# Sums of moving operands kept in DRAM, fewer plain blocks at an operand change, and a split that comes two steps after its fetch

## The chip, the core and the metric

The kernel runs on one core of one Trainium2 chip. The metric is the device time of one execution in microseconds (us); the time quoted for a kernel is the median of several executions. All matrix products are made by TensorE (PE), which reads both operands from on-chip memory and writes to PSUM; VectorE (DVE), ScalarE (ACT) and GpSimd (POOL) do the rest; SyncE (SP) issues nearly all DMA transfers, in one queue and in order.

## The reference, cut to what matters

One transformer-like layer over 2048 tokens of width 1024, all in float32: a token mixer, a cross-attention into 256 memory tokens, and a SwiGLU feed-forward part, each between two RMS norms.

```python
def reference(x, mem, w_in, sinks, ...):
        ...
        y = jnp.concatenate([ya, yh.astype(ya.dtype)], axis=-1) @ w_out[l]
        h = h + rms_norm(y, g_mix_post[l])
        u = rms_norm(h, g_x_pre[l])
        m = rms_norm(mem, g_mem[l])
        y = cross_attention(u, m, wq_x[l], wk_x[l], wv_x[l], wo_x[l])
        h = h + rms_norm(y, g_x_post[l])
        u = rms_norm(h, g_ffn_pre[l])
        y = (jax.nn.silu(u @ w_gate[l]) * (u @ w_up[l])) @ w_down[l]
        h = h + rms_norm(y, g_ffn_post[l])
```

The lines shown are those that the changed stage computes; the input projection, the sliding-window attention and the recurrence come before it and are not touched.

## The kernel before

Every float32 operand is split into a high and a low part, and a product is made of three matmuls (high by high, high by low, low by high; L950, L951 and L952). The high part is a rounding copy on ACT (L870), the low part a subtraction on DVE (L873).

The later part of the kernel is a chain of eight *jobs* (`jobs`, L1158). A job is one matrix product whose *moving* operand (called T here) stays the same while a row of *blocks* runs over tokens or columns. A block is a product of a 2x2 arrangement of stationary tiles S with the 2x2 arrangement of T, 256 rows by 1024 columns of output. The jobs in order, with the names used below:

| name | moving operand from | k tiles per quarter (`nk`) | blocks |
|---|---|---|---|
| w_out | the output projection | 4 | 8 |
| qk | `qk_d`, a folded product of weights | 4 | 8 |
| vo | `vo_d`, another one | 4 | 8 |
| u0, u1 | `u_d`, the normed tokens 0 to 1023, then 1024 to 2047 | 4 | 22 each |
| d0, d1, d2 | `w_down`, in three parts | 3, 4, 4 | 8 each |

A block is made in one of two ways (`STEPS`, L863). A *plain* block ("p", function `eight`) makes the eight quarter products from the four quarters of T, under the keys 1, 2, 8 and 3. An "s" block (function `seven`) makes the same output from seven products; its T operands are the quarters 1, 2 and 3 and four sums of quarters, under the keys 5, 7, 6 and 4, used in the order 1, 5, 6, 3, 7, 2, 4. One product is 3 x `nk` matmuls into one PSUM bank; it is called a step below.

`kinds` (L1180) makes the first block of every job plain (the first two of w_out) and the last one too, but for the very last block of the kernel. Between jobs the T operands must be exchanged: there are seven slots for them in on-chip memory (L1045), and a slot is free when its operand was used for the last time. Since the last block of a job is plain, the slots of the four sums come free before it, and the four quarters' slots during it. `half` (L1063) is called after every step of a block (twice after a step of a plain block) and makes half an operand: in `resident` (L875) it fetches one or two tiles of 512 KB into *row* tiles (nine of them for all uses, `row_tile`, L1196), for a sum makes a `tensor_tensor` on DVE (L887 for key 5, L890 for 7, L893 for 6, L896 for 4), and splits the result on ACT and DVE (L870, L873). Keys 6 and 4 reuse the sum made for 7 and 6, and key 7 is taken out of turn, five steps early (L1044), for that. So nine operands are made at a change: the quarter 8 for the old job's last block, the four quarters of the new job's plain block, and the four sums.

All this is traced in the order of the Python code; a scheduler then orders the instructions of each engine, so that a split may stand earlier or later among the others than it was written. Each engine takes its instructions strictly in that order: an instruction that waits holds up all that stand behind it. SP's queue holds the loads of T, the loads of S (`streamed`, L903), and the stores of results. In w_out, vo, d1 and d2 a result tile is first added to by an accumulating DMA that POOL issues (`add`), and its store on SP waits for that transfer.

Of the kernel before, what the change touches and what calls it, by code (L numbers as in the profile page):

```python
# [11 lines left out]
F32 = mybir.dt.float32  # L12
# [3 lines left out]
ALU = mybir.AluOpType  # L16
AX = mybir.AxisListType

P = 128
T = 2048  # L20
D = 1024
# [4 lines left out]
NFF = DFF // P  # L26
# [3 lines left out]
NT = T // P  # L30
# [18 lines left out]
class Layer:  # L49
# [27 lines left out]
    def store(self, dst, src):  # L77
        self.nc.sync.dma_start(dst, src)

    def gain(self, ap):  # L80
        self._n += 1
        g = self.gp.tile([P, D], F32, tag="g", name=f"g_{self._n}")
        self.load(g, ap[0:1, :].broadcast_to([P, D]))
        return g
# [316 lines left out]
    def in_first(self):  # L401

        nc, I = self.nc, self.I
# [12 lines left out]
        T, raw = {}, {}  # L416
# [47 lines left out]
        def fetch():  # L464
            for s in range(2):
                for q in range(2):
# [9 lines left out]
                  for i, p in enumerate(self.ORDER)]  # L476
        phases = self.phases([(lambda i, j, a, n: raw[i, j][:, a:a + n, :], 4, blocks)], T)
        next(phases)
# [395 lines left out]

    def resident(self, get, nk, key, dst, keep):  # L875


        nc = self.nc
        halves = [(0, (nk + 1) // 2), ((nk + 1) // 2, nk)]

        src = []
        for h, (a, b) in enumerate(halves):
            if key in self.BLOCK:
                t = get(*self.BLOCK[key], a, b - a)
            elif key == 5:
                t, o = get(0, 1, a, b - a), get(0, 0, a, b - a)
                nc.vector.tensor_tensor(t, t, o, ALU.subtract)  # L887
            elif key == 7:
                t, o = get(1, 1, a, b - a), get(0, 1, a, b - a)
                nc.vector.tensor_tensor(t, t, o, ALU.subtract)  # L890
            elif key == 6:
                t, o = keep[7][h], get(0, 0, a, b - a)
                nc.vector.tensor_tensor(t, t, o, ALU.add)  # L893
            else:
                t = get(1, 0, a, b - a)
                nc.vector.tensor_tensor(t, t, keep[6][h], ALU.subtract)  # L896
            self.split2(t, dst[:, 0, a:b], dst[:, 1, a:b], "A")
            src.append(t)
            yield
        if key in (6, 7):  # L900
            keep[key] = src

# [128 lines left out]
    def phases(self, jobs, first, prologue=None):  # L1031

        steps = [(n, i, p) for n, (_, nk, blocks) in enumerate(jobs) for i, b in enumerate(blocks)
                 for p in self.STEPS[b[0]]]
        takes = [c for _, _, blocks in jobs for b in blocks for c in self.TAKES[b[0]]]
        need = list(itertools.accumulate(takes)) + [sum(takes)] * 2
# [8 lines left out]
        current = [None, 0]  # L1047
        if first:
            for i, p in enumerate(first):
                k = (0, p, False)  # L1050
                queue.remove(k)
                T[k] = first[p]
                slots[i] = ("A", uses[k][-1], i)

        def fetch(n, tile):
            def get(i, j, a, c):
                t = tile().rearrange("p (k d) -> p k d", d=512)[:, :c]
                jobs[n][0](t, i, j, a, c)
                return t

            return jobs[n][0] if first else get

        def half(g, tile):  # L1063

            if current[0] is None:
# [12 lines left out]
                T[k] = dst  # L1078
                current[:] = [self.resident(fetch(n, tile), jobs[n][1], p, dst, keep[n]), 0]
            next(current[0])  # L1080
            current[1] += 1
            if current[1] == 2:
                next(current[0], None)
                current[0] = None
            return True

        blocks = [b for _, _, bl in jobs for b in bl]
        streams, ready, made = [], [], [0]
# [15 lines left out]
        if not first:  # L1104
            for i in range(8):
                half(-1, prologue)
                yield
        stream(0)
# [6 lines left out]
        at = 0  # L1115
        for n, (_, nk, bl) in enumerate(jobs):
            for i, (kind, _, out, follow, addend) in enumerate(bl):
                stream(at + 1)
                cur = {}
                for q in range(g, g + len(self.STEPS[kind])):  # L1120
                    key = (n, steps[q][2], i > len(bl) // 2 if steps[q][2] == 8 else 0)
                    while key not in T or (current[0] is not None and key == list(T)[-1]):
                        assert half(q - 1, self.row_tile), (q, steps[q], queue[:3], slots)
                    cur[steps[q][2]] = T[key]
                run = (self.seven(ready, cur, nk, out, addend) if kind == "s" else
                       self.eight(ready, cur, nk, out, addend, kind == "q"))
                for q in range(len(self.STEPS[kind])):
                    next(run)
                    upto(need[g + 2])
                    for _ in range(1 if kind == "s" else 2):  # L1130
                        for f in list(after):
                            if next(f, after) is after:
                                after.remove(f)
                        half(g, self.row_tile)
                    g += 1
                after.append(follow())
                at += 1
# [20 lines left out]
    def jobs(self):  # L1158
# [24 lines left out]
        jobs = [(w_out, 4, kinds([self.mixed_block(n) for n in range(0, NT, 2)], 2)),  # L1183
                (weights(self.qk_d, 0, 4), 4, kinds([self.score_block(n) for n in range(0, NT, 2)])),
                (weights(self.vo_d, 0, 4), 4, kinds([self.value_block(n) for n in range(0, NT, 2)]))]
        for b in range(NB):
            jobs.append((ffn_u(b), 4, kinds([blk for f in range(0, NFF, 2) for blk in self.hidden_blocks(b, f)])))
        for c, (f0, nk) in enumerate(((0, 3), (6, 4), (14, 4))):
            jobs.append((weights(I["w_down"], f0 * P, nk), nk,
                         kinds([self.down_block(c, f0, nk, n) for n in range(0, NT, 2)])))  # L1190
        k, s, o, f, a = jobs[-1][2][-1]
# [122 lines left out]
    def value_block(self, n):  # L1314
# [3 lines left out]
        def out(i, j, a, b):  # L1318
            if not y:
                ss.append(self.small("q_s", 4))  # L1320
            if i not in y:
                y[i] = self.row_tile()
                if n == 0 and len(y) == 1:
                    self.g_x_post = self.gain(self.I["g_x_post"])
                    self.g_ffn_pre = self.st_pool.tile([P, D], F32, name="g_ffn_pre", bufs=1)
                    self.load(self.g_ffn_pre, self.I["g_ffn_pre"][0:1, :].broadcast_to([P, D]))
# [157 lines left out]
```

## Time and profile before

| | us |
|---|---|
| median of 3 executions | 2679.54 (2676.87 to 2679.78) |
| the profiled execution | 2676.9 |
| its span, first to last instruction | 2675.0 |
| TensorE busy in it | 2587.2 (97%) |
| VectorE busy | 1688.1 (63%) |
| ScalarE busy | 1239.6 (46%) |
| GpSimd busy | 489.3 (18%) |

The profile is a page on one execution and a trace that can be asked for views. In a row of a *view of windows* stand the stretch (us from the start), its length, then the busy time of PE, of PE's weight loads, of DVE, ACT and POOL with the number of instructions in brackets, the granted TensorE clock (1.00 is full speed), the busy share of the 16 DMA engines (slightly over 1 is possible) and GB/s. In a row of a *view of groups* stand line, engine, operation, names and shapes, the count, busy us, the mean ns of one, and the idle time of the engine before them. A busy PE is not a PE at its peak: matmuls overlap in the records, so the number of matmuls in a stretch says more than its busy time.

### The profile page before, as it was taken

To read this page: it belongs to the slowest core of one execution; us is meant where nothing else is said; L and a number is where in the kernel's file an instruction comes from. 1 tells how busy PE (TensorE), PEld (TensorE's weight loads), DVE (VectorE), ACT (ScalarE), POOL (GpSimd) and SP (SyncE) were. 2 spreads that over 40 slices of the span, in tenths; PEclk is the share of its full clock that TensorE was granted. 3 is DMA by queue.
4 is the path that set the end of the run, shared out by engine and by line. 5 is a ranking of instruction groups with operands and counts; after the bars stand their busy time and mean duration, and the time that the engine had idled before them with its cause. 6 is when DMAs were issued, how large, how long until landed. Compare 5 with 4: busy or idle time off the path is not lost.

```text
span 2675.0 us, 34685 instructions
## 1 busy us (share of the span) xinstructions
PE 2587.2 (97%) x12410; PEld 2163.8 (81%) x12410; DVE 1688.1 (63%) x2643; ACT 1239.6 (46%) x2589; POOL 489.3 (18%) x675
## 2 busy tenths in 40 slices
PE   7989999999988998999989999999999999999998
PEld 6877888888987887888868888888888888888786
DVE  7675488777544657677666555575555556574666
ACT  5453366655423565565554333343333344443443
POOL 4241344332431332223320000000000000000022
PEclk9999999999999999999999999999999999999999
DMA  5435655446877797377793222262222245586988
GB/s 181 149 127 170 182 160 150 140 136 171 239 233 231 196 263 226 105 250 193 212 287 111 78 80 86 90 234 93 87 87 77 81 133 184 197 246 178 290 210 218
DMA packets 394412, 452.25 MB, mean 169 GB/s; under 512 B 19072, under 2 KB 309888, under 8 KB 394240
## 3 DMA queue, kind: packets, MB, share of 16 engines
q1 hardware_dynamic: 383584, 411.25, 48.0%
q0 software_dynamic: 10656, 38.80, 8.2%
q8 instruction: 97, 1.59, 0.2%
q14 instruction: 75, 0.61, 0.1%
HBM read 315.77 MB, written 134.22 MB: 168 GB/s over the span
## 4 chain that ended last, share of the span: by engine, by line
PE 79%; DMA 10%; DVE 4%; POOL 3%; issue 2%; ACT 2%; SPq 1%; POOLq 0%; DVEq 0%; ACTq 0%
PE psm L952 21%; PE psm L950 21%; PE psm L951 21%; PE psg L153 3%; PE psg L152 3%; PE psg L151 3%; DMA row<-in_w_down_dram 1%; PE pss L1151 1%; DMA row<-in_w_out_dram 1%; DMA row<-h_d 1%; DMA row<-in_x_dram 1%; DMA row<-qk_d 1%; DMA z<-in_w_out_dram 1%; DMA raw<-in_wo_x_dram 1%; DMA row<-u_d 1%
## 5 line engine op out<-in xcount | busy, mean ns | idle before, releaser
L950 PE MATMUL psm<-T,S 128*128 128x512 f32 x2726 | 1060.7, 393 | 23.2 <-ACT part L965 12.4
L951 PE MATMUL psm<-T,S 128*128 128x512 f32 x2726 | 1066.4, 391 | 0.5 <-DVE T L873 0.5
L952 PE MATMUL psm<-T,S 128*128 128x512 f32 x2726 | 1057.1, 391 | 2.5 <-DVE S L873 2.5
L950 PEld LDWEIGHTS psm<-T,S 128*128 128x128 f32 x2726 | 514.9, 189 | 133.2 <-ACT part L965 14.5
L952 PEld LDWEIGHTS psm<-T,S 128*128 128x128 f32 x2726 | 514.5, 189 | 111.0 <-DVE S L873 4.2
L951 PEld LDWEIGHTS psm<-T,S 128*128 128x128 f32 x2726 | 514.7, 189 | 106.7 <-DVE T L873 1.2
L873 DVE TENSOR_TENSOR S<-sraw,S 128x512 fp32r<-128x512 f32 (+1 forms) x327 | 227.6, 701 | 253.1 <-ACT S L870 233.8
L870 ACT ACTIVATE S<-sum 128x512 fp32r<-128x512 f32 (+1 forms) x288 | 172.8, 619 | 329.0 <-PE psm L952 233.4
L873 DVE TENSOR_TENSOR S<-sum,S 128x512 fp32r<-128x512 f32 (+1 forms) x340 | 229.1, 684 | 62.0 <-ACT S L870 39.1
L965 ACT ACTIVATE part<-psm 128x512 f32<-128x512 f32 x249 | 147.4, 597 | 224.8 <-PE psm L952 209.5
L1243 POOL DMA_DIRECT2D row<-y_d x28 | 25.9, 925 | 1138.9 <-DMA sraw<-hid_d 971.8
L870 ACT ACTIVATE S<-sraw 128x512 fp32r<-128x512 f32 (+1 forms) x274 | 168.8, 617 | 125.1 <-PE psm L952 113.2
L873 DVE TENSOR_TENSOR T<-row,T 128x1024 fp32r<-128x1024 f32 (+1 forms) x134 | 158.4, 1190 | 76.0 <-ACT T L870 75.1
L870 ACT ACTIVATE T<-row 128x1024 fp32r<-128x1024 f32 (+1 forms) x134 | 137.6, 1033 | 132.0 <-DVE row L887 35.7
L151 PE MATMUL psg<-u,whi 128*128 128x512 f32 x352 | 141.8, 403 | 1.6 <-POOL whi L135 1.6
L153 PE MATMUL psg<-u,wlo 128*128 128x512 f32 x352 | 140.2, 398 | 0.9 <-DVE wlo L136 0.9
L152 PE MATMUL psg<-u,whi 128*128 128x512 f32 x352 | 139.9, 397 | 0.0
L1214 ACT ACTIVATE junk<-row 128x512 f32<-128x512 f32 x160 | 99.9, 626 | 58.7 <-DVE row L1236 17.5
L1366 DVE TENSOR_TENSOR row<-psm,part 128x512 f32<-128x512 f32 x60 | 39.9, 688 | 68.5 <-PE psm L952 68.5
L136 DVE TENSOR_TENSOR wlo<-raw,whi 128x1024 fp32r<-128x1024 f32 x46 | 60.4, 1312 | 35.9 <-POOL whi L135 35.8
L1375 DVE TENSOR_TENSOR part<-psm,part 128x512 f32<-128x512 f32 x60 | 39.7, 688 | 63.8 <-PE psm L952 63.8
L135 POOL TENSOR_SCALAR whi<-raw 128x1024 fp32r<-128x1024 f32 x46 | 53.6, 1166 | 135.1 <-PE psg L152 34.7
(334 smaller groups left out, 3626.4 us busy)
## 6 DMA issues: line engine op xcount, KB each, us to landing
row<-in_w_down_dram SPq DMA_DIRECT2D x53, 512.0 KB, 7.1
sraw<-in_w_gate_dram SPq DMA_DIRECT2D x44, 512.0 KB, 3.8
sraw<-in_w_up_dram SPq DMA_DIRECT2D x44, 512.0 KB, 3.8
row<-u_d SPq DMA_DIRECT2D x44, 512.0 KB, 7.5
hid_d<-row SPq DMA_DIRECT2D x44, 512.0 KB, 2.6
h_d<-row SPq DMA_DIRECT2D x32, 512.0 KB, 5.4
y_d<-row SPq DMA_DIRECT2D x32, 512.0 KB, 3.0
sraw<-hid_d SPq DMA_DIRECT2D x32, 512.0 KB, 5.3
```

The lines of the kernel that those rows point to most:

```text
L135: nc.gpsimd.tensor_scalar(hi, raw, 1.0, 1.0, ALU.mult, ALU.mult)
L136: (lo_engine or nc.vector).tensor_tensor(lo, raw, f32(hi), ALU.subtract)
L151: nc.tensor.matmul(ps, ah, bh, start=(i == 0), stop=False)
L152: nc.tensor.matmul(ps, ah, bl, start=False, stop=False)
L153: nc.tensor.matmul(ps, al, bh, start=False, stop=(i == n - 1))
L870: self.nc.scalar.activation(hi, raw, AF.Copy)
L873: self.nc.vector.tensor_tensor(lo, raw, f32(hi), ALU.subtract)
L950: nc.tensor.matmul(ps, s[:, 0, k, :], t[:, 0, k, :], start=st, stop=False, **kw)
L951: nc.tensor.matmul(ps, s[:, 0, k, :], t[:, 1, k, :], start=False, stop=False, **kw)
L952: nc.tensor.matmul(ps, s[:, 1, k, :], t[:, 0, k, :], start=False, stop=sp, **kw)
L965: nc.scalar.activation(t, ps, AF.Copy)
L1214: self.nc.scalar.activation(junk, a, AF.Square, scale=float(D) ** -0.5, accum_out=to)
```

## The change

Three things are changed in the chain of jobs.

*Plain blocks.* `kinds` now takes no plain first block as its default. w_out keeps two, qk and u0 one each. vo, u1, d0, d1 and d2 begin with an "s" block. Key 8 is then made once in those jobs, for the last block.

*Sums in DRAM.* For those five jobs a new helper, `combined`, makes the four sums 7, 6, 4 and 5 during the job before (vo's in block 1 of qk and after, u1's from block 4 of u0, those of d0, d1 and d2 one after the other from block 2 of u1). For each half of T it fetches quarters into two tiles that are not row tiles (the tile of the gains, and the tile that held `g_ffn_pre`), makes four `tensor_tensor` on DVE, and stores the four results. `resident` then fetches a sum as it fetches a quarter, with no arithmetic. In the old way the sums stay in w_out, qk and u0.

*Fetch and split apart.* `half` now only issues the fetches and notes the split; the split is issued two steps later for the quarters, and for the sums where they come from DRAM. It is traced inside `behind`, which orders it on ACT and DVE behind the instructions that those engines had when the step's products were issued. `Ready` makes an operand on demand when a block asks for one that isn't complete.

```diff
-    def resident(self, get, nk, key, dst, keep):
+    def resident(self, get, nk, key, dst, keep, sums):
...
+        def fetched(a, b):
+            if key in self.BLOCK:
+                return get(*self.BLOCK[key], a, b - a), None
+            if sums:
+                return get(key, None, a, b - a), None
+            if key == 5:
+                return get(0, 1, a, b - a), get(0, 0, a, b - a)
...
+        def split(a, b, t, o):
+            if o is not None:
+                nc.vector.tensor_tensor(t, t, o, ALU.add if key == 6 else ALU.subtract)
+            self.split2(t, dst[:, 0, a:b], dst[:, 1, a:b], "A")
...
+            yield lambda a=a, b=b, t=t, o=o: split(a, b, t, o)
+
+    def combined(self, get, nk, dst):
+
+        nc = self.nc
+        halves = [(0, (nk + 1) // 2), ((nk + 1) // 2, nk)]
+        for a, b in halves:
+            def put(key, t, o, op):
+                with self.behind():
+                    nc.vector.tensor_tensor(t, t, o, op)
+                self.store(dst[self.CHAIN.index(key), :, a * 512:b * 512], t.rearrange("p k d -> p (k d)"))
+
+            for x, y in (((1, 1, 7), (0, 1, 0)), (None, (0, 0, 6)), (None, (1, 0, 4)), ((0, 1, 5), (0, 0, 0))):
+                if x:
+                    key, op, t = x[2], ALU.subtract, get(0, *x[:2], a, b - a)
+                o = get(1, *y[:2], a, b - a)
+                for _ in range(4):
+                    yield
...
+    @contextlib.contextmanager
+    def behind(self):
+
+        with contextlib.ExitStack() as at:
+            for e in (mybir.EngineType.Activation, mybir.EngineType.DVE):
+                if self.last.get(e) is not None:
+                    at.enter_context(self.tc.issue_after(self.last[e]))
             yield
...
-        queue = sorted(uses, key=lambda k: (uses[k][0] - (5 if k[1] == 7 else 0), k))
+        queue = sorted(uses, key=lambda k: (uses[k][0] - (5 if k[1] == 7 and jobs[k[0]][3] is None else 0), k))
...
+        def lag(k):
+            return 2 if k[1] in self.BLOCK or jobs[k[0]][3] is not None else 0
+
+        def split(g):
+
+            if pending and pending[0][0] <= g:
+                _, k, f = pending.pop(0)
+                f()
+                left[k] -= 1
+                return True
+            return False
...
+            k, f = current[0]
+            pending.append((g + lag(k), k, next(f)))
...
+                        if pending and lag(pending[0][1]):
+                            with self.behind():
+                                split(g)
+                        else:
+                            split(g)
                         half(g, self.row_tile)
...
-        def kinds(blocks, n=1):
+        def kinds(blocks, n=0):
...
+        vo_s, u_s = sums("vo_s", vo, 4), sums("u_s", ffn_u(1), 4)
+        d_s = [sums(f"d_s{c}", src, nk) for c, (src, _, nk) in enumerate(down)]
+        jobs = [(w_out, 4, kinds([self.mixed_block(n) for n in range(0, NT, 2)], 2), None, {}),
+                (qk, 4, kinds([self.score_block(n) for n in range(0, NT, 2)], 1), None, {1: [vo_s[1]]}),
+                (vo, 4, kinds([self.value_block(n) for n in range(0, NT, 2)]), vo_s[0], {})]
         for b in range(NB):
...
+            beside = {2: [in_turn(*(d[1] for d in d_s))]} if b else {4: [u_s[1]]}
+            jobs.append((ffn_u(b), 4, kinds([blk for f in range(0, NFF, 2) for blk in self.hidden_blocks(b, f)], 1 - b),
+                         u_s[0] if b else None, beside))
+        for c, (src, f0, nk) in enumerate(down):
+            jobs.append((src, nk, kinds([self.down_block(c, f0, nk, n) for n in range(0, NT, 2)]), d_s[c][0], {}))
```

More of the change, by code (lines that the diff above doesn't have):

```diff
@@ L1106, in phases @@
                 half(-1, prologue)
+                split(len(steps))
                 yield
@@ L1115, in phases @@
         at = 0
-        for n, (_, nk, bl) in enumerate(jobs):
+        self.last = {}
+        for _, nk, bl, _, beside in jobs:
             for i, (kind, _, out, follow, addend) in enumerate(bl):
                 stream(at + 1)
[L1119 to L1126, printed above, removed]
+                after += [f() for f in beside.get(i, ())]
+                run = (self.seven(ready, Ready(), nk, out, addend) if kind == "s" else
+                       self.eight(ready, Ready(), nk, out, addend, kind == "q"))
                 for q in range(len(self.STEPS[kind])):
                     next(run)
+                    self.mark()
                     upto(need[g + 2])
@@ L1186, in jobs, with sums, get @@
-        for b in range(NB):
[L1187 to L1190, printed above, removed]
+        def sums(name, src, nk):
+            dst = self.tc.dram_tile([4, P, nk * 512], F32, name=name)
+            def get(which, i, j, k0, n):
+                t = (self.gain_tile, self.extra_tile)[which]().rearrange("p (k d) -> p k d", d=512)[:, :n]
+                src(t, i, j, k0, n)
+                return t
+            return dst, lambda: self.combined(get, nk, dst)
```

90 lines of the change are left out of this document (57 added, 33 removed).

## The prediction

> **What bounds the kernel now.** I read the page first, then a view of windows over the jobs and their changes, then the chain of waits and SP's waits at the change to d2, the worst that the diff rewrites.
>
> ```profile
> span 2675.0 us, 34685 instructions
> PE 2587.2 (97%) x12410; PEld 2163.8 (81%) x12410; DVE 1688.1 (63%) x2643; ACT 1239.6 (46%) x2589; POOL 489.3 (18%) x675
> ...
> PE 79%; DMA 10%; DVE 4%; POOL 3%; issue 2%; ACT 2%; SPq 1%; POOLq 0%; DVEq 0%; ACTq 0%
> ```
>
> The chain that ends last is 79% TensorE. So a matmul taken away is time taken away, and the rest of the chain (DMA 10%, DVE 4%) is where the PE is made to wait. The windows say where:
>
> ```profile
> 1450.00:1750.00 300.00, 300.00 (x1325) 248.47 (x1325) 166.74 (x255) 107.70 (x191) 0.00 (x0) 1.00 0.27 86
> 1060.00:1150.00 90.00, 90.00 (x435) 75.25 (x434) 62.05 (x126) 50.21 (x127) 21.28 (x33) 1.00 0.38 112
> 1025.00:1045.00 20.00, 12.79 (x48) 9.38 (x47) 18.28 (x30) 15.74 (x38) 6.79 (x8) 0.74 0.76 249
> 1180.00:1205.00 25.00, 25.00 (x120) 20.80 (x119) 20.43 (x29) 14.26 (x28) 4.54 (x4) 1.00 0.78 248
> 1350.00:1405.00 55.00, 44.06 (x185) 34.86 (x183) 35.20 (x38) 32.82 (x65) 12.77 (x16) 0.91 0.90 277
> 1785.00:1810.00 25.00, 25.00 (x112) 20.68 (x112) 24.25 (x28) 12.58 (x16) 0.00 (x0) 1.00 1.05 374
> 2215.00:2240.00 25.00, 25.00 (x112) 20.68 (x112) 19.34 (x29) 10.40 (x16) 0.00 (x0) 1.00 0.60 198
> 2340.00:2360.00 20.00, 20.00 (x90) 16.58 (x89) 14.09 (x17) 9.33 (x13) 0.00 (x0) 1.00 1.05 386
> 2360.00:2380.00 20.00, 20.00 (x90) 16.57 (x89) 19.42 (x23) 11.73 (x17) 1.79 (x2) 1.00 0.81 236
> 2500.00:2525.00 25.00, 25.00 (x112) 20.72 (x111) 13.10 (x13) 8.94 (x12) 1.75 (x2) 1.00 1.05 346
> 2525.00:2540.00 15.00, 9.86 (x33) 7.61 (x32) 14.06 (x17) 8.89 (x14) 1.75 (x2) 0.77 0.76 184
> ```
>
> The first row is the steady state (u0): 300 us for 1325 matmuls, 226.4 ns each, with DVE busy 56% and DMA 27%. The second is the middle of qk. The others are changes. At 226.4 ns, a stretch that holds fewer matmuls has lost the difference: into qk (1025 to 1045) 88.3 would fit and 48 stand, 9.1 us lost; into u0 (1350 to 1405) 242.9 against 185, 13.1 us; into d2 (2525 to 2540) 66.3 against 33, 7.5 us. Together 29.7 us. The changes into vo (1180), u1 (1785), d0 (2215) and d1 (2340) lose nothing that can be seen: 112 matmuls in 25 us is the full pace. Yet DVE is busy 24.25 of 25 us at u1 and 19.42 of 20 at d1: there, operands are made far enough ahead that a full DVE doesn't show. That lead is what the change spends.
>
> ```profile
> 2498.79 6.54 DMA row<-in_w_down_dram
> 2505.45 1.24 DVE row L890
> 2506.70 13.55 DMA row<-in_w_down_dram
> 2520.38 1.24 DVE row L887
> 2521.64 1.07 ACT T L870
> 2522.73 1.23 DVE T L873
> ...
> 2534.28 0.79 PE psm L950
> 2535.07 0.43 PE psm L951
> ```
>
> ```profile
> SPq L78 <- DMA row<-y_d: 23.2, 4, 9.0
> ...
> row<-in_w_down_dram SPq DMA_DIRECT2D x20, 512.0 KB, 8.8
> ```
>
> This is how d2 loses its 7.5 us. SP stood up to 9.0 us at a store that waits for its accumulating transfer, the loads of T behind it then went out in a burst (DMA share 1.05), one of them was 13.55 us on its way, DVE stood at the sum of key 5 and 7, and all that queues behind it on DVE came late. The stalled changes (qk, u0, d2) are just those where the ending job (w_out, vo, d1) has such stores; at the four others there are none.
>
> **The change, part by part.**
>
> *Fewer products.* A plain block has eight products, an "s" block seven. Five first blocks change; four have 12 matmuls to a product, d0's has 9: 4 x 12 + 9 = 57 matmuls less (in the built order the two kernels differ by just 57). They lie in PE's stream, so 57 x 226.4 ns = **-12.9 us**.
>
> *Arithmetic at the change.*
>
> ```profile
> L870 ACT ACTIVATE T<-row 128x1024 fp32r<-128x1024 f32 x125 | 132.3, 1062 | 131.6 <-DVE row L887 35.7 <-DMA row<-in_w_down_dram 27.1 <-DVE row L890 25.8
> L873 DVE TENSOR_TENSOR T<-row,T 128x1024 fp32r<-128x1024 f32 x125 | 152.3, 1226 | 75.4 <-ACT T L870 74.5
> L887 DVE TENSOR_TENSOR row<-row,row 128x1024 f32<-128x1024 f32 x15 | 18.3, 1222 | 20.4 <-DMA row<-in_w_down_dram 6.0 <-DMA row<-u_d 5.5 <-DMA row<-qk_d 5.3
> L873 DVE TENSOR_TENSOR S<-sraw,S 128x512 fp32r<-128x512 f32 x301 | 213.2, 713 | 233.5 <-ACT S L870 214.3 <-POOL S L872 18.8
> ```
>
> At each of the five changes eight sums of 1.22 us leave (9.8 us of DVE), one operand is made less (2 x 1.23 us), and the "s" block adds three S splits at 0.71, four sums of S and three evictions of the same shape, taken at the same 0.7 (7 us): net 5 us less for DVE. The time is 0 of itself, since PE bounds; with PE's cover gone it would be a gain of up to 5 us a change, which can't be had where nothing is lost. The sums reappear in the job before: 9.8 us of DVE for vo in qk, where DVE is busy 62.05 of 90 us, and 39 us in u0 and u1, where it idles 44%. Cost **0**; if each of the 40 held up an S split by its whole 1.22 us, 49 us, but S has five buffers, so two steps (5.4 us) of lead: I keep 0 to +3.
>
> *DMA.* A job's change needs 16 tile loads instead of 22 (two per operand, eight operands; before, nine and four more for the sums). `combined` adds 12 loads and 8 stores per job, elsewhere: 100 transfers, which at 374 GB/s (the u1 row) take 1.4 us each, in stretches where the share is 0.27 and 0.38. Cost **0**, with one exception below. SP issues them too, and stands at each reuse of the two tiles until a store has landed (5.0 us for `pt_d` stores, next fence); the S loads behind it are a block ahead. 0.
>
> *The lead.* The text says that operands are fetched two steps ahead; in the built order the loads stand where they stood, relative to the job's end, and the splits stand later. I counted, for each operand, the steps between the last product whose eviction stands ahead of its split on ACT or DVE and its first use. For vo's 1, 2, 8, 3, then 5, 6, 4 it was 10, 10, 12, 11, 7, 7, 9; for 1, 5, 6, 3, 7, 2, 4 it is now 7, 6, 7, 4, 3, 2, 3. u1 ends on 3, 1, 1, d1 on 3, 2, 3, d2 on 3, 2, 2. The last operand waits for a slot until the plain block ends, and is used seven products on: 19 us for a load, two steps, two ACT and two DVE passes.
>
> ```profile
> row<-vo_d SPq DMA_DIRECT2D x20, 512.0 KB, 6.2
> pt_d<-row SPq DMA_DIRECT2D x6, 512.0 KB, 5.0
> 1318.00:1326.00 8.00, 7.01 (x35) 5.46 (x34) 6.05 (x7) 6.29 (x12) 2.26 (x5) 1.00 0.48 141
> ```
>
> The price of a late operand isn't in the trace, so I bound it per change: 0 (the four changes today) to 7.5 us (d2 today). Lead against need: the second half of key 2 in vo is issued 4.5 steps = 12.2 us before use; 6.2 us to land and 1.06 + 1.23 for the split leave 3.7 us. But in vo SP first stands at the store of the very last sum (key 5, second half), because the load of that sum is next but one; that takes 5 us as a `pt_d` store does, and it's the exception above. So vo is short by about 1.3 us, and a late split stands ahead of S splits: I take **+3**. d1: its plain block's steps are of 9 matmuls (2.0 us), 16 loads in about 16 steps, DVE nearly full: **+2**. u1 and d0: 8 loads in 2.5 steps, then quiet (share 0.60 at d0); each **+0.5**. Sum +6, bounds 0 to 30.
>
> *d2.* Its 7.5 us come from loads behind stores and from DVE standing at two-tile sums. The first stays; six of 22 loads go; but seven operands are wanted in the first seven steps. Between -7.5 and +7.5; I take **-3**. *qk and u0* keep plain blocks and their sums; the quarters' splits now stand where their loads have more often landed. u0's key 5 still waits behind two `h2_d` stores. Between -6 and +4 together; I take **-1**.
>
> Sum: -12.9 + 6 - 3 - 1 = **-10.9 us**. The profiled execution took 2676.9 us (1.9 around its span), so 2666.0; it is the fastest of three and 2.6 under their median of 2679.5, so I predict a median of 2668.6, rounded to **2669**.
>
> A rule of the Trainium skill speaks against small stalls being small: the page TensorE: Matmul & The Clock Gate, section Part 1: The HAM clock gate, says that a PE idle for a window of about 3.4 us falls to half rate and stays there for about as long. The traces agree: after d2's gap matmuls stand 0.43 us apart instead of 0.23 and the clock row reads 0.77, while a gap of about a microsecond (1318 to 1326) leaves 1.00. By the rule vo's 3 us would cost nothing more or, if it grew just over the window, 1.7 us more; the sum would be -10.9 or -9.2.
>
> **The rivals.**
>
> *B, given back.* Each of the four quiet changes pays the break-even 12.9/4 = 3.2 us, d2 stays at 7.5: 0, so 2679. For it: DVE 24.25 of 25 us at u1 even with the long lead. Against: DVE has 5 us less to do there and 6 loads fewer.
>
> *C, slower.* The last operands, 2 and 4, come late at every change of the five. Place: ACT's and DVE's queues, where a split that waits for its load holds up the S splits and evictions behind it, so that PE stands and then runs at half clock. Price: d2's 7.5 us, at vo, u1, d0 and d1 too: 4 x 7.5 - 12.9 = +17, 2697; at 5 us each +7, 2687. It decides from a mean of 3.2 us on. For it: leads of 1 to 3 steps, and 8.8 us to land in the busy stretch of d2. Against: without accumulates on the ending job SP isn't held, and at u1 and d0 loads have quiet queues.
>
> *D, larger gain.* d2's stall and a third of u0's (4 us) go with the waits of ACT and DVE for loads, and nothing new appears: -12.9 - 7.5 - 4 = -24, 2655. For it: the rows of d2 above put the wait on DVE's sums. Against: SP's 9.0 us stay.
>
> *E, the edit does nothing.* The products counted in the built order exclude it for the 57 matmuls; for the fetch it is half true, as said, and counted.
>
> **How the numbers follow.** Forecast A (2657 to 2674) 0.55, B 0.18, C 0.19, D 0.08. A difference under 0.2% (5.4 us) can't be told from none here: faster means under 2674.2, slower over 2684.9. A and D are all faster: 0.63. B spans 2674 to 2685: same 0.18. C is slower: 0.19. The range: low end -12.9 with d2's stall gone and qk and u0 2 better, 2657, leaving out most of D (0.07); high end 2686, leaving out the upper part of C (0.12).
>
> **What would show it.** Matmuls L950 to L952 fall by 57 in total. Around the first step of vo and d1 a view of windows lacks some 13 matmuls (3 us) and 9 (2 us) of the full pace of 112 in 25 us; u1 and d0 lack at most 2. `row<-row,row` groups lose 40 instructions, and the same number appears on two other tiles before the changes. d2's change lacks about 20 (4.5 us) instead of 33. I am wrong if one of the four quiet changes loses more than 5 us, with ACT's T split ended by a DMA in the view of waits; if u0 or qk moves by more than 5 us; or if S splits come late in qk or u1 outside the changes.

## The result and the profile after

| | before | after |
|---|---|---|
| median, us | 2679.66 (2676.87 to 2681.99, 4 executions) | 2655.28 (2651.22 to 2659.56, 4 executions) |
| the profiled execution | 2676.9 | 2655.67 |
| its span | 2675.0 | 2653.9 |

The ratio of the medians is 0.991, 95% interval 0.9891 to 0.9928: faster by 24.4 us where 10.9 were forecast, and 1.7 us below the low end of the range. Two later sets with the same kernel gave 0.9916 (0.9901 to 0.9931) and 0.9918 (0.9904 to 0.9933).

The head of the page after, the busy row and the shares of the chain that ended last:

```profile
span 2653.9 us, 34808 instructions
...
PE 2571.9 (97%) x12353; PEld 2151.1 (81%) x12353; DVE 1703.6 (64%) x2683; ACT 1238.5 (47%) x2597; POOL 485.4 (18%) x675
...
PE 79%; DMA 8%; DVE 4%; POOL 3%; issue 3%; ACT 2%; SPq 1%; POOLq 0%; DVEq 0%; ACTq 0%
```

TensorE still sets the end, with 57 matmuls fewer (12410 to 12353), as counted ahead. The windows of the new kernel, columns as before, first the steady state of u0 and the middle of qk, then the changes into qk, vo, u0, u1, d0, d1 and d2, and a stretch inside d2:

```profile
1450.00:1750.00 300.00, 300.00 (x1325) 248.43 (x1324) 173.57 (x261) 107.86 (x190) 0.00 (x0) 1.00 0.38 122
1060.00:1150.00 90.00, 90.00 (x434) 75.14 (x434) 66.73 (x132) 48.35 (x124) 24.98 (x33) 1.00 0.69 206
1000.00:1045.00 45.00, 37.83 (x163) 29.38 (x162) 34.22 (x45) 26.91 (x57) 14.07 (x20) 0.92 0.91 304
1180.00:1215.00 35.00, 33.77 (x158) 27.12 (x156) 29.07 (x44) 23.06 (x45) 10.69 (x9) 1.00 0.60 186
1350.00:1405.00 55.00, 45.13 (x194) 35.68 (x193) 39.19 (x41) 33.62 (x61) 5.62 (x11) 0.94 0.88 275
1785.00:1810.00 25.00, 25.00 (x112) 20.71 (x111) 20.60 (x26) 13.18 (x20) 0.00 (x0) 1.00 0.62 205
2205.00:2235.00 30.00, 30.00 (x134) 24.86 (x133) 22.87 (x37) 13.72 (x24) 0.00 (x0) 1.00 0.48 157
2325.00:2355.00 30.00, 30.00 (x134) 24.84 (x133) 27.86 (x35) 23.12 (x33) 0.92 (x1) 1.00 0.79 279
2480.00:2525.00 45.00, 45.00 (x200) 37.26 (x199) 31.43 (x40) 26.71 (x44) 4.62 (x7) 1.00 0.82 244
2590.00:2620.00 30.00, 28.20 (x124) 22.70 (x123) 18.97 (x29) 11.62 (x25) 5.57 (x8) 1.00 0.98 247
```

u0's middle holds the same 1325 matmuls in 300 us, though DVE and the DMA queues carry the new sums (255 to 261 DVE instructions, a DMA share of 0.27 to 0.38). At u1, d0, d1 and d2 the count is the full pace of 226.4 ns: d2's 45 us would fit 198.8 and hold 200. The 33 matmuls missing at d2 before are there. At vo PE is idle 1.2 us, at qk and u0 it still stands, and inside d2 a loss is new.

To compare whole kernels I counted PE's lost time: the start-to-start times of successive matmuls, as far as they exceed the median for their shape. For single changes they are summed in stretches of 10 us, and only stretches over 0.8 us are counted. Before it is 139.6 us in all, after 132.0, of which some 78 us lie ahead of 780 us in both. So 12.9 us of matmuls and 7.6 us of waiting make 20.5 of the 21.1 us between the two spans. The remaining 3 us of the 24.4 are that the profiled execution of before was 2.8 us under its median and that of after 0.4 above.

### The profile page after: what moved, and what is told of

Same layout as the page of the kernel before. It is cut to its first block, busy times and chain, and to the rows that moved or that the text cites. A ratio compares the mean times of both kernels' runs of the same rounds, so it can differ in the third digit from the quotient of the medians.

```text
span 2653.9 us, 34808 instructions
## 1 busy us (share of the span) xinstructions
PE 2571.9 (97%) x12353; PEld 2151.1 (81%) x12353; DVE 1703.6 (64%) x2683; ACT 1238.5 (47%) x2597; POOL 485.4 (18%) x675
## 4 chain that ended last, share of the span: by engine, by line
PE 79%; DMA 8%; DVE 4%; POOL 3%; issue 3%; ACT 2%; SPq 1%; POOLq 0%; DVEq 0%; ACTq 0%
PE psm L1004 21%; PE psm L1005 21%; PE psm L1006 21%; PE psg L160 2%; PE psg L159 2%; PE psg L158 2%; PE pss L1239 1%; DMA row<-in_w_out_dram 1%; DMA row<-h_d 1%; DMA raw<-in_wo_x_dram 1%; DVE wlo L143 1%; POOL whi L142 1%; DMA row<-in_x_dram 1%; SPq L75 1%; DMA raw<-in_wv_x_dram 0%
## 5 line engine op out<-in xcount | busy, mean ns | idle before, releaser
L877 ACT ACTIVATE S<-sum 128x512 fp32r<-128x512 f32 (+1 forms) x306 | 183.8, 619 | 341.4 <-PE psm L1006 249.2
L880 DVE TENSOR_TENSOR S<-sum,S 128x512 fp32r<-128x512 f32 (+1 forms) x360 | 242.3, 683 | 64.6 <-ACT S L877 41.9
L1019 ACT ACTIVATE part<-psm 128x512 f32<-128x512 f32 x264 | 156.6, 597 | 244.9 <-PE psm L1006 228.2
L880 DVE TENSOR_TENSOR T<-row,T 128x1024 fp32r<-128x1024 f32 (+1 forms) x124 | 145.3, 1187 | 59.0 <-ACT T L877 58.7
L877 ACT ACTIVATE T<-row 128x1024 fp32r<-128x1024 f32 x124 | 124.4, 1030 | 47.2 <-DVE row L906 36.2
L979 DVE TENSOR_TENSOR sum<-sraw,sraw 128x512 f32<-128x512 f32 (+1 forms) x90 | 62.2, 691 | 30.9 <-DMA sraw<-in_w_in_dram 6.8
L879 POOL TENSOR_SCALAR S<-sum 128x512 fp32r<-128x512 f32 x54 | 44.9, 831 | 188.1 <-PE psm L1006 144.8
```

The lines of the kernel that those rows point to most:

```text
L877: self.nc.scalar.activation(hi, raw, AF.Copy)
L880: self.nc.vector.tensor_tensor(lo, raw, f32(hi), ALU.subtract)
L979: nc.vector.tensor_tensor(t, a, b, op)
L1019: nc.scalar.activation(t, ps, AF.Copy)
```

## The experiments

All times of a table row were taken with the kernel before on the same chip, so the ratio is what is compared between rows. "Lost" is the count just described, of the profiled execution.

| kernel | median, us | ratio (95%) | lost | qk | vo | u0 | d1 | d2 | inside d2 |
|---|---|---|---|---|---|---|---|---|---|
| before | | 1 | 139.6 | 11.2 | 0 | 16.5 | 0 | 7.9 | 1.1 |
| lead alone, plain kept | 2674.68 | 0.9999 (0.9988 to 1.0011) | 138.9 | 10.4 | 3.8 | 12.3 | 0 | 8.1 | 1.1 |
| sums alone, plain kept | 2669.73 | 0.9954 (0.9935 to 0.9973) | 133.2 | 12.6 | 0 | 14.5 | 0 | 0.9 | 1.1 |
| sums and lead, plain kept | 2664.01 | 0.9958 (0.994 to 0.9976) | 128.0 | 12.3 | 0 | 12.6 | 0 | 0 | 1.0 |
| plain gone alone | 2677.29 | 0.9992 (0.9979 to 1.0004) | 161.5 | 10.7 | 6.0 | 15.1 | 6.3 | 8.9 | 3.1 |
| plain gone, lead | 2673.83 | 0.9987 (0.9976 to 0.9998) | 152.2 | 12.3 | 5.4 | 11.9 | 7.4 | 7.0 | 3.3 |
| plain gone, sums | 2669.08 | 0.9973 (0.9959 to 0.9986) | 145.1 | 11.9 | 7.2 | 14.7 | 2.7 | 5.5 | 1.1 |
| after (all three) | 2655.28 | 0.991 (0.9891 to 0.9928) | 132.0 | 11.1 | 1.3 | 14.1 | 0 | 0 | 3.3 |

u1 and d0 have no column: they lose nothing over 0.8 us but in "plain gone, lead", where it is 1.0 and 2.0 us. These eight are the change taken apart. "Plain" is the plain first block of vo, u1, d0, d1 and d2; "sums" are those kept in DRAM; "lead" is the split issued two steps behind its fetch.

**No lead (plain gone, sums).** In the loop over steps:

```diff
-                        if pending and lag(pending[0][1]):
-                            with self.behind():
-                                split(g)
-                        else:
-                            split(g)
                         half(g, self.row_tile)
+                        split(len(steps))
```

> The changed kernel with each split issued right behind its fetch, as before, not two steps later. Theory S: within 3 us of the changed kernel, 2654 to 2659. Theory L: ACT and DVE stand at loads again, d2 loses its 7.9 us and the quiet changes, whose leads are shorter now, more than that together: 2665 to 2685.

**Sums at the change (plain gone, lead).** No `combined`, no DRAM sums; the quarters keep their two steps:

```diff
-                (vo, 4, kinds([self.value_block(n) for n in range(0, NT, 2)]), vo_s[0], {})]
+                (vo, 4, kinds([self.value_block(n) for n in range(0, NT, 2)]), None, {})]
...
-            beside = {2: [in_turn(*(d[1] for d in d_s))]} if b else {4: [u_s[1]]}
+            beside = {}
...
```

> The changed kernel with the sums of vo, u1, d0, d1 and d2 made at the change again, on DVE, from two fetched tiles; the plain first blocks stay away, the quarters keep their lag of two steps. Theory S (the sums from DRAM took d2's stall away and keep the quiet changes quiet): d2's 7.9 us come back, and vo, u1, d0 and d1 lose 3 to 8 us each, 2675 to 2695. Theory L (it was the later split): some 3 us over the changed kernel, 2658 to 2662.

Neither theory holds alone: without the lead the ratio is 0.9973, without the sums 0.9987, and each time most of the gain is lost. The view of PE's and ACT's waits at d2 of the kernel without a lead (engine, tile and line, what it waited for, then us in all, times, longest):

```profile
PE psm L1004 <- ACT part L1019: 4.2, 1, 4.2
...
ACT T L877 <- DMA row<-d_s: 9.7, 5, 5.6
ACT T L877 <- DMA row<-in_w_down_dram: 2.4, 2, 1.2
```

PE doesn't wait for a T here. It waits for a PSUM bank that ACT must empty (L1019), and ACT stands ahead of that at splits whose loads have not landed. At vo of that kernel the order alone is enough: ACT works without a wait from 1190.7 us on, first at two T splits (2.0 us) and then at a result row, and comes only at 1193.7 to the eviction L1019 that PE waits for. In the changed kernel the same view of ACT over 2480 to 2525 us reads:

```profile
ACT part L1019 <- PE psm L1006: 7.5, 5, 2.9
ACT S L877 <- PE psm L1006: 6.1, 4, 1.9
ACT row L1525 <- PE psm L1006: 3.7, 2, 2.1
ACT T L877 <- DMA row<-d_s: 0.7, 1, 0.7
```

Now ACT waits for PE, and for a load only 0.7 us. Without the sums in DRAM the lead doesn't help, since then what the split waits for is DVE's arithmetic. d1 in that kernel, its window and the waits of PE and ACT:

```profile
2330.00:2360.00 30.00, 25.67 (x101) 19.89 (x100) 26.64 (x30) 21.30 (x30) 0.00 (x0) 0.89 0.86 311
...
PE psm L1004 <- ACT T L877: 3.3, 2, 2.2
...
ACT T L877 <- DVE row L906: 6.2, 2, 5.5
```

DVE is busy 26.6 of 30 us and PE stands for T itself: seven operands, four with a sum, are wanted in the first seven steps. In the changed kernel DVE is as busy at d1 (27.9 of 30 us) and PE loses nothing, so a full DVE alone does not make this loss.

**With the plain blocks kept.** The lead alone, the sums alone, and both (the last two also with `kinds(..., 1)` for the five jobs, as here for d0 to d2):

```diff
-            jobs.append((src, nk, kinds([self.down_block(c, f0, nk, n) for n in range(0, NT, 2)]), d_s[c][0], {}))
+            jobs.append((src, nk, kinds([self.down_block(c, f0, nk, n) for n in range(0, NT, 2)], 1), d_s[c][0], {}))
```

> The kernel before with the later split of the quarters alone: plain first blocks kept, sums made at the change, nothing in DRAM. Theory S: as the kernel before within 3 us, 2676 to 2680, with d2's stall of 7.9 us in place. Theory L: d2's stall goes, and u0's shrinks, 2667 to 2672.

> The changed kernel with a plain first block in vo, u1, d0, d1 and d2 again (57 matmuls more), sums from DRAM and lag kept. If the seven-product first block costs nothing at the changes: 12.9 us over the changed kernel, 2668. If the leads of 1 to 3 steps do cost what I had put down (6 us at the quiet changes): 2661 to 2663. Under theory S and L alike d2 doesn't stall.

> The changed kernel with plain first blocks kept and no lead: sums kept in DRAM, but each half divided right behind its fetch. It is the fourth of the combinations with plain blocks: before (neither), lead alone 0.9999, both 0.9958. Theory J (sums and lead are worth something only together): 0.998 to 1.001, with d2 still losing 4 to 8 us. Theory I (with plain blocks the sums alone do it, as VectorE is relieved of the 40 sums at the changes): 0.995 to 0.997, nothing lost at d2.

The lead alone does nothing. The sums alone take d2's 7.9 us to 0.9 (theory I), and with a plain block ahead the lead adds nothing that the intervals can tell. Sums in DRAM also mean four loads less at a change with a plain block (18 instead of 22); no run parts this from the arithmetic that goes. Sums and lead with the plain blocks, 0.9958, lie 0.0048 or some 12.8 us above the changed kernel, about what 57 matmuls take. At d2 of the kernel with the sums alone, its window, then ACT's waits, then SP's from 2455 to 2520 us:

```profile
2500.00:2530.00 30.00, 29.97 (x133) 24.48 (x131) 14.62 (x16) 15.21 (x21) 2.67 (x4) 1.00 0.90 290
...
ACT T L877 <- DMA row<-d_s: 10.9, 3, 8.4
ACT T L877 <- DMA row<-in_w_down_dram: 5.3, 1, 5.3
...
SPq L78 <- DMA row<-y_d: 45.8, 7, 9.9
```

SP stands at its stores for 45.8 us in that stretch, and ACT stands 16.2 us for loads that come behind them; yet 133 matmuls fill the 30 us. So with a plain block there is time for a load that is late, if nothing more has to be done to it than the split.

**The last corner, and half the lead.** Plain blocks gone with neither of the others (the two edits above together), and the changed kernel with `return 1` for `return 2` in `lag`:

> The last of the eight combinations: the five plain first blocks gone as in the changed kernel, but sums formed at the change and no lead (with the lead alone it was 0.9987). Theory H (a change without a plain block needs seven operands in 21 us instead of four in 11, so ScalarE's queue stands at late divisions with PE's evictions behind; the lead helps only where the sums come ready): 0.998 to 1.001, 20 to 30 us of PE lost at the five changes against the 12.9 us saved. Theory G (the lead alone does half of it): above 1.002.

> The changed kernel with a lead of one step instead of two. With none it was 0.9973, with two 0.991. Theory P (margins of 0 to 2 us at the last operands are real, a step of 2.7 us is all that keeps the divisions from standing): 0.993 to 0.9955, 3 to 8 us lost at vo and d2. Theory Z (any order that puts the divisions behind the step's evictions does it, since SP's issue is hardly moved): 0.9905 to 0.9925.

Plain gone alone is 0.9992: 22 us more are lost (161.5 against 139.6), which eats the 12.9 (its profiled execution was the longest of ten, so the count is on the high side). Theory H. One step of lead gives 2659.19 us, 0.9926 (0.9911 to 0.994), nearer to two steps than theory P had it, but with the losses that P names: 3.9 us at d2 and 2.0 at vo. No run has the new order without a step of lead, so how much is due to the order and how much to the first step stays open.

**d2 alone as before.** A plain first block for d2, its sums formed at the change, no lead for its operands; the other four as in the changed kernel:

```diff
-            jobs.append((src, nk, kinds([self.down_block(c, f0, nk, n) for n in range(0, NT, 2)]), d_s[c][0], {}))
+            jobs.append((src, nk, kinds([self.down_block(c, f0, nk, n) for n in range(0, NT, 2)], c // 2),
+                         None if c == 2 else d_s[c][0], {}))
...
+            if k[0] == len(jobs) - 1:
+                return 0
...
```

> The changed kernel, but its last change (into the third job of the down projection, d2) is as it was before: a plain first block, its sums formed from fetched quarters at the change, each half divided right behind its fetch. Theory S (the sums in DRAM with the two steps of lead are what took away the stall of 7.9 us at d2): that stall comes back whole, plus 12 matmuls of 226 ns (2.7 us): about 10 us above the changed kernel, a ratio of 0.9945 to 0.996 to the kernel before, and 6 to 9 us of PE's lost time again within some 30 us of the change. Theory A (the stall had its cause in what the earlier jobs did, such as later stores and fetches that pile up, which the change moved): only the 2.7 us come back, a ratio of 0.991 to 0.993, no stall at d2. Kept in any case: SP's stand at stores behind accumulating transfers.

2663.72 us, ratio 0.9938 (0.9923 to 0.9953). PE lost 8.0 us at d2 again (theory S); the ratio is a little under S's, in part since the loss inside d2 went down to 1.1 us. So d2's own arrangement makes its stall: what the earlier jobs leave behind is as in the changed kernel, where d2 loses nothing.

**SP's stand.** The prediction put d2's stall down to SP standing at stores that wait for accumulating transfers. In the kernel before, the store of the second down job was moved some calls behind its accumulate; in the changed kernel the same was done in w_out, vo and d1:

```diff
-                if not last:
+                if not last and not c:
                     self.store(self.y2_d[(n + i) * P:(n + i + 1) * P, :], y[i])
                 yield
+            if c and not last:
+                yield
+                yield
+                for i in range(2):
+                    self.store(self.y2_d[(n + i) * P:(n + i + 1) * P, :], y[i])
+                    yield
```

> The kernel before, with one edit: in the down projection's second job the store of a summed row tile is issued three to four calls after its accumulating transfer instead of right behind it, so that SP does not stand at it with the next job's operand fetches queued behind. Theory Q (the prediction's: SP's stand at these stores bunches the fetches and makes d2's stall of 7.9 us): the stall falls to 0 to 3 us, 2667 to 2672 by a before of 2675, ratio 0.997 to 0.999. Theory V (the stall comes from VectorE's four two-tile sums and late divisions at the change, SP's stand is hidden): SP's waits for y_d shrink from 36 us to under 10 in the window ahead of d2, but PE still loses 6 to 9 us there; ratio 0.999 to 1.001.

> The changed kernel with the stores of row tiles behind accumulating transfers (w_out, vo and d1 jobs) issued three calls later, so that SP no longer stands at them. Theory Q (SP's stand delays fetches on the changes into qk, u0 and d2): the 11 and 14 us that PE loses in qk and u0 fall by 3 or more each, ratio 0.985 to 0.989. Theory V (SP's stand is hidden; what PE waits for is ScalarE's queue): 0.990 to 0.9925, the waits for the accumulating transfers smaller, PE's loss the same.

> The changed kernel once more, for the comparison with the kernel with later stores: 0.991 to 0.992 of the kernel before.

> The changed kernel with the stores behind accumulating transfers three calls later, once more. Theory V (SP's stand is hidden): within 0.1% of the changed kernel in this set. Theory Q (the stand costs PE something): 0.15% or more below it.

The kernel before with later stores took 2674.76 us against 2677.37, ratio 0.999 (0.9978 to 1.0001). But SP's stand hardly changed: over the whole kernel SP stands 93.4 us at stores behind `y_d` transfers before, and 90.3 us with later stores. Ahead of d2 theory V expected under 10 us. The next lines are from this kernel: first SP's waits in the 65 us that end some 9 us ahead of PE's stall at d2 (2449 to 2514 us), then PE's and ACT's at the change.

```profile
SPq L78 <- DMA row<-y_d: 29.9, 4, 9.6
...
PE psm L950 <- ACT part L965: 4.7, 1, 4.7
...
ACT T L870 <- DVE row L887: 7.1, 2, 6.6
ACT T L870 <- DVE row L890: 5.4, 1, 5.4
```

Without the edit the first line reads 33.1 us. The loads came no earlier either: in the 45 us around the change DVE's sums waited 9.7 us for them, against 6.7 us before. PE still lost 7.3 us, and ACT waited for DVE's sums as before.

The changed kernel with later stores first seemed 4.6 us better than its control (0.9908 against 0.9916); in a set with more executions both took the same, 2655.70 and 2655.61 us, ratios 0.992 (0.9908 to 0.9932) and 0.9918. Here too the stand is as it was: behind the transfers from `x` (w_out) 61.2 us against 61.3, from `h_d` 145.7 against 144.1, from `y_d` 90.3 against 89.4. So these runs say nothing on SP's stand, for theory Q or for V; a kernel without such a stand was not made.

What does say something is the stand in kernels that differ at d2 in other ways. SP's waits in a stretch of 65 us ahead of the change, in the kernel before (2455 to 2520 us), the one with d2 alone as before (2440 to 2505) and the changed kernel (2440 to 2505):

```profile
SPq L78 <- DMA row<-y_d: 33.1, 5, 9.9
...
SPq L78 <- DMA row<-y_d: 32.3, 5, 9.6
...
SPq L78 <- DMA row<-y_d: 32.1, 7, 9.2
```

PE loses 7.9, 8.0 and 0 us there; with the sums alone the stand is 45.8 us and the loss 0.9. So a stand of this size does not make the stall by itself. Whether it has a part in it while the sums are formed at the change is not shown.

**One change more.** The sums of qk made in DRAM while w_out runs, no plain first block in qk:

```diff
...
-        jobs = [(w_out, 4, kinds([self.mixed_block(n) for n in range(0, NT, 2)], 2), None, {}),
-                (qk, 4, kinds([self.score_block(n) for n in range(0, NT, 2)], 1), None, {1: [vo_s[1]]}),
+        qk_s = sums("qk_s", qk, 4, (self.extra_tile, self.row_tile))
+        jobs = [(w_out, 4, kinds([self.mixed_block(n) for n in range(0, NT, 2)], 2), None, {1: [qk_s[1]]}),
+                (qk, 4, kinds([self.score_block(n) for n in range(0, NT, 2)]), qk_s[0], {1: [vo_s[1]]}),
```

> The changed kernel, and the same for one change more: the sums of the qk operand are made while the w_out job runs, from its second block on, and kept in DRAM; no plain first block in qk; its halves divided two steps behind their fetch. Theory E (a change to operands that are fetched as finished sums costs PE nothing, wherever it is): the 12 matmuls (2.7 us) go and of the 11 us that PE loses around 1000 to 1045 us 5 to 10: ratio 0.986 to 0.989, 7 to 12 us under the changed kernel. Theory W (the loss there is one of transposes, of ScalarE and of the rows of the w_out job, with VectorE 0.9 full): 2.7 us go at most, ratio 0.990 to 0.9915, or the added sums in w_out cost as much as they save.

2657.96 us, ratio 0.9923 (0.9902 to 0.9944): no gain over the changed kernel. The profiled execution was the longest of four, 7.5 us over the median, so its waits are on the high side. The change into qk, its window and the waits of PE and ACT in that kernel:

```profile
1000.00:1045.00 45.00, 33.95 (x139) 26.72 (x138) 25.45 (x30) 26.41 (x55) 9.03 (x16) 0.89 0.97 294
...
PE psm L1004 <- ACT T L877: 5.4, 1, 5.4
...
ACT T L877 <- DMA row<-qk_d: 5.8, 1, 5.8
```

139 matmuls where the changed kernel has 163. DVE has less to do (25.45 against 34.22 us), so the sums are gone from the change; but a quarter comes late, and with no plain block PE stands at it 5.4 us. Theory E falls: at qk a change to finished sums is not free, because a load comes late.

**Control.** The changed kernel beside the third set:

> The changed kernel itself, beside the other kernels of this set: 0.9905 to 0.9925 of the kernel before, PE's lost time as in its first profile (none at vo, u1, d0, d1, d2 but 1 to 2 us).

2656.94 us, ratio 0.9916; 133.4 us lost in all, with qk 12.0, vo 1.1, u0 13.1, d1 and d2 0, inside d2 3.8. So single entries of the table repeat to about 1 us.

## Why the prediction failed, step by step

*Fewer products, -12.9: right.* 57 matmuls went. The spans of the kernels follow products and lost time together: plain gone with sums, 5.5 us more lost and 12.9 us of products, should be 7.4 us under 2675.0, and its span is 2666.8.

*Arithmetic and DMA at no cost: right, as far as the windows show.* The groups of DVE that now make the sums of the five jobs, beside the old way's:

```profile
L924 DVE TENSOR_TENSOR g<-g,extra 128x1024 f32<-128x1024 f32 x27 | 32.9, 1219 | 12.7 <-DMA extra<-in_w_down_dram 6.5 <-DMA g<-in_w_down_dram 2.7 <-issue 1.7
L906 DVE TENSOR_TENSOR row<-row,row 128x1024 f32<-128x1024 f32 x24 | 29.7, 1236 | 26.2 <-DMA row<-in_w_out_dram 23.2 <-DMA row<-qk_d 1.6 <-DMA h1t_d<-row 1.4
...
L924 DVE TENSOR_TENSOR extra<-extra,g 128x1024 f32<-128x1024 f32 x9 | 11.0, 1219 | 0.5 <-DMA extra<-vo_d 0.3 <-DMA extra<-in_w_down_dram 0.2
```

With four of half the size they are 40, and as many left the rows' groups; the windows of u0 and qk above show no price for them.

*d2, "The first stays; ... I take -3": wrong, and this is the step that failed.* Measured: -7.9, which is 4.9 of the 9.6 us by which the sum missed. The prediction held SP's stand for the stall's first cause and DVE's sums for a follow-up, so it let only a part go. The timeline of the kernel before, five instructions on three engines (start, us, what, and in brackets the idle time before it and its releaser), shows what released PE:

```profile
2520.38 1.23 DVE L887 TENSOR_TENSOR row<-row,row 128x1024 f32<-128x1024 f32 x1 [3.14 <-DMA row<-in_w_down_dram]
...
2531.43 2.35 DVE L896 TENSOR_TENSOR row<-row,row 128x1024 f32<-128x1024 f32 x2
...
2532.68 1.06 ACT L870 ACTIVATE T<-row 128x1024 fp32r<-128x1024 f32 x1 [2.14 <-DVE row L896]
2533.64 0.58 ACT L965 ACTIVATE part<-psm 128x512 f32<-128x512 f32 x1
...
2534.28 0.79 PE L950 MATMUL psm<-T,S 128*128 128x512 f32 x1 [5.14 <-ACT part L965]
```

The load for the first of these sums landed at 2520.3 us. The loads for the next three landed at 2523.0, 2524.3 and 2528.0, each at least 1.4 us before its sum began, so these sums waited for DVE and not for a load. From 2520.4 us to the release DVE had no gap over 1.1 us, and 4.9 us of its work were sums (L887, L893 twice, L896 once). The split of key 4 waited for the last of them, the eviction L965 stood behind that split on ACT, and PE behind the eviction. The chain of waits quoted in the prediction already held these sums and the split, and in it even the load of 13.55 us begins where the sum L890 ends, not where a store does; the prediction took the sums for what follows a late load, not for what sets the release. The runs bear this out: with a stand of 45.8 us and loads that ACT waited 16.2 us for, finished sums left 0.9 us of the stall, and d2 put back brought back 8.0 us under the same stand as in the changed kernel. After the wait PE ran at half pace: twelve matmuls 0.43 us apart, 2.4 us, so 5.3 + 2.4 make 7.7 of the 7.9 us.

*The lead, +6 for the quiet changes: mis-sized.* Measured +1.3, all at vo (PE waits 1.2 us for T); that is another 4.7 us of the miss. What was feared is real where there is no lead: 7.2 us at vo and 2.7 at d1 then. I had priced a late split by what stands behind it ("a late split stands ahead of S splits"). But the new order puts it behind the step's evictions and splits. ACT waits only 0.7 us for loads at d2, and at vo what is late is one T alone. SP's stand in vo that I counted in for +3 did occur:

```profile
SPq L78 <- DVE extra L924: 4.3, 1, 4.3
SPq L75 <- DMA vo_s<-extra: 2.6, 1, 2.6
SPq L75 <- DMA vo_s<-g: 2.3, 1, 2.3
```

PE's whole wait at vo is 1.2 us, so it cost no more than that.

*qk and u0, -1: about right.* -2.5, 2.4 of it at u0, inside the bounds of -6 to +4; the control gives -2.6. The remark that the stalled changes are just those whose ending job has such stores was not tested, since no run took SP's stand away. What the cause is stays open. The sums that they still form at the change are the nearest: ACT's T splits wait for them 14.2 us around qk and 5.1 us around u0 in the changed kernel. But at qk moving them only moved the wait to a load.

*Not foreseen: inside d2, +2.2.* Between 2590 and 2620 us the chain of waits now contains an accumulating transfer:

```profile
2590.71 11.59 DMA row<-y_d
```

The DMA share is 0.98 there, but it is 0.96 at the same place of the kernel before, and 1.00 with one step of lead, where nothing is lost. In the runs the loss never shows where d2 has its plain block, and it shows in most kernels without one, though not in those with the sums and no lead or one step of it. Why was not tested and stays open.

The sum by measured terms is -12.9 - 7.9 + 1.3 - 2.5 + 2.2 = -19.8, and with small losses elsewhere (-0.7) the 20.5 above, against -10.9. Rival D named the time, 2655, and for d2 the right mechanism: its stall goes whole. That the time fits to the microsecond is partly luck, for D gave u0 4 us where 2.4 came, and had neither the 1.3 us at vo nor the 2.2 inside d2. It had 0.08 because SP's 9.0 us "stay". Stands of up to 9.2 us did stay ahead of d2, and PE lost nothing there.

## What to carry to other kernels

When an engine waits, ask first what stands in front of it in the releaser's own queue, and follow every piece of work between the late load and the release. A queue that stands for long at a store may be hidden. A run that is meant to take a wait away should be read for that wait first: here the moved stores left SP's stand as it was, and their times answered nothing. Edits that are worth nothing alone may be worth much on top of another: the lead alone gives 0.9999 and the plain blocks' going alone 0.9992, but with the sums in DRAM the two together bring 0.9954 to 0.991, some 12 us. Operands finished ahead of time shorten what follows a late load, the lead keeps a late load from holding the queue, and in this kernel only both made it safe to take the cover (the plain block) away. A split that waits for its load belongs behind the evictions of its step.

## What the hardware showed

The gate of TensorE's clock. At vo of the kernel without a lead, PE's timeline and the window behind the wait:

```profile
1190.12 0.39 PE L1006 MATMUL psm<-T,S 128*128 128x512 f32 x1
1194.33 0.79 PE L1004 MATMUL psm<-T,S 128*128 128x512 f32 x1 [3.82 <-ACT part L1019]
1194.93 0.63 PE L1005 MATMUL psm<-T,S 128*128 128x512 f32 x1
...
1194.30:1197.30 3.00, 2.97 (x7) 2.39 (x8) 3.00 (x8) 1.94 (x3) 0.00 (x0) 0.51 0.00 0
1197.30:1201.00 3.70, 3.70 (x21) 3.08 (x21) 3.64 (x8) 2.10 (x4) 0.00 (x0) 1.00 0.45 138
```

Between 1194.3 and 1197.3 us the granted clock is 0.51 with 7 matmuls, 0.43 us apart; from 1197.3 on it is 1.00 and they come 0.23 us apart. So 3.8 us of waiting cost about 1.4 us more, close to the 1.7 us estimated in the prediction. The Trainium skill, page TensorE: Matmul & The Clock Gate, section Part 1: The HAM clock gate (the "warmup" mystery), gives one busy window of about 3.4 us for the way back and says that the window runs freely; the traces agree roughly: 3.0 us of half pace here, 5.3 us behind d2's wait in the kernel before (twelve matmuls 0.43 us apart, 2534.28 to 2539.56). But in the changed kernel at qk a recorded wait of 3.0 us was enough, and half pace lasted longer there, its window:

```profile
1034.00:1041.00 7.00, 5.75 (x13) 3.76 (x14) 7.00 (x13) 5.86 (x12) 1.58 (x2) 0.53 0.51 162
```

13 matmuls in 7 us at 0.53, with two more short waits in it (0.21 and 0.69 us). Yet at u0 of the same kernel a wait of 3.1 us (to 1366.6 us) left the clock at 1.00:

```profile
1366.50:1370.00 3.50, 3.44 (x20) 3.00 (x20) 3.50 (x4) 1.09 (x2) 0.93 (x1) 1.00 0.86 260
```

The wait at qk had two others, of 0.65 and 0.70 us, in the 3 us ahead of it, this one at u0 had none. A later one at u0, of 3.2 us (to 1391.7 us) and again with others just ahead, was followed by a clock of 0.50 (1392.5 to 1398.8 us). So a wait of about 3 us may cost the clock or not; what decides was not tested. The prediction's "gap of about a microsecond" that left the clock at 1.00 is two waits, of 0.55 and 0.44 us, 1.2 us apart.
